# Up-projection token operands formed without GpSimd arithmetic, and halves of all tiles squared and scaled early for the last norms

## The chip, the cores and the metric

The kernel runs on one core of one Trainium2 chip. The metric is the device time of one execution in microseconds (us), which is a little longer than the span from the first to the last profiled instruction. The engines are called by their short names here: PE is TensorE's matmul and PEld its weight load, DVE is VectorE, ACT is ScalarE, POOL is GpSimd, SP is SyncE. SP issues plain DMAs, POOL issues those that add to their destination.

## The reference, cut to what matters

One layer of an encoder on 1024 tokens of 1024 channels, then a last norm. The change is in the norms and in the feed-forward part; the three mixers are left out here.

```
def rmsnorm(x, g):
    inv = lax.rsqrt(jnp.mean(xf * xf, axis=-1, keepdims=True) + RMS_EPS)
    return xf * inv * g

h = h + ymix @ w_out
h = h + conv_ffn(rmsnorm(h, norm2_g), w_up, ffn_conv_w, ffn_conv_b, w_down)   # 1024 -> 2 x 2816 -> 1024
return rmsnorm(h, final_norm_g)

def conv_ffn(h, w_up, conv_w, conv_b, w_down):
    u = dwconv_centred(h @ w_up, conv_w, conv_b)      # width 3 along the tokens
    a, v = jnp.split(u, 2, axis=-1)
    return (jax.nn.gelu(a) * v) @ w_down
```

## The kernel before, in words

**Precision.** Every large product is made in three matmuls (`mm3`, L97): an operand is split into a high part, which ACT writes rounded (L87), and a low part, the rest, by one subtraction (L88, on DVE unless another engine is named). `dsplit` is the other way to the same pair: ACT writes the negated value into the low part, a DMA issued by POOL adds the value to it (L93), and ACT then writes the high part.

**Tokens.** The residual lives in eight tiles `h` of 128 tokens by 1024 channels. After the mixers each tile is normed (`normed`, by `token_rstd`: two squares with accumulated sums on ACT, `tot` and `ms` on DVE, a power on POOL, a scaling on DVE).

**Up-projection.** It is a Strassen-Winograd product: seven half-size products instead of eight for each of 22 blocks `j` of 128 gate and 128 value channels. Its token operands are B11 and B21 (made from tiles 0 to 3 by `Ffn.first`), and B22, T1 to T4 (made by `Ffn.second` for four channel groups `kt` from transposes on PE that land in PSUM banks `trp`). There are four single banks, and a set of transposes takes a bank each. T1 is B12 minus B11, T2 is B22 minus T1, T3 is B12 minus B22, T4 is B21 minus T2. Its weight operands are made by `gate(j)` and `value(j)`: two loads, four sums and differences of 128x512 (L1208 to L1211), and the splits into A1, A22, S2 and S3. `start(j)` makes products P1 and P2 (`p` in the profile, p1 and p2 here), `rest(j)` P3, P6, P7, P5, P4 in this order, and puts them together on DVE (L1247 to L1259); then come the convolution (L712, L718), the gelu and a product on POOL (L1265). A product is 12 matmuls of 128x512.

**The order.** PE's instructions stand in the order in which the program issues them. On DVE, ACT, POOL and SP a scheduler orders them when the program is built, by its own view of time and by given priorities. The program calls `start(0)`, one group of `second` after each of its two products, the same with `start(1)`, then `start(2)`, then `rest(0)`. The raw halves of `second` (b22, t1, t2, t3) and z share six buffers of 128x512.

**Down-projection.** Again Strassen-Winograd, in two chunks `c` of seven products `p` with 6 and 5 steps: each step splits two blocks (tiles `dw`, on ACT and DVE) and uses them for four token tiles. Between them stand the sums of blocks (L1305) and the evacuations of PSUM into `h` (L1370). At the end of the second chunk, product 5 finishes the upper right half of tiles 0 to 3, which are then normed and stored (`final`), and the right half of tiles 4 to 7 is squared and multiplied by the gain on POOL (`done`, L1377). Product 6 finishes the left half of tiles 4 to 7, and `last` norms and stores them.

## Time and profile before

| | |
|---|---|
| time, median of 3 runs | 1168.62 us (1168.1 to 1172.08) |
| profiled execution | 1171.44 us, span 1169.7 us |
| PE | 1080.7 us, 92% of the span |
| PEld | 876.9 us, 75% |
| DVE | 988.4 us, 85% |
| ACT | 545.3 us, 47% |
| POOL | 338.2 us, 29% |
| granted TensorE clock, mean | 0.963 of full speed |

Busy shares are averages over very different stages. The up-projection's operands are made from about 479 to 528 us, the blocks run until about 930 us, the down-projection until the end. "Idle before, <-" in a row names what ended the engine's wait just before the group, with the time waited; x is the number of instructions.

### The profile page before, as it was taken

The page shows a single profiled execution, that of the slowest core. Times are in us where ns is not written, and L with a number is a line of the kernel's source. Part 1 is how long each engine was busy: PE and PEld are TensorE (multiplying, and loading weights), DVE is VectorE, ACT ScalarE, POOL GpSimd, SP SyncE. Part 2 cuts the span into 40 slices and gives each one's busy share as a digit, 9 for nine tenths or more (in the row PEclk, how much of TensorE's full clock was granted, in tenths as well). Part 3 has the DMA queues.
Part 4 walks back from the last instruction along what each step waited for, and adds up shares of the span by engine and source line. Part 5 has one row for each costly group of instructions (what it writes and reads, how often), then busy time and mean ns, then how long its engine had stood idle before and what let it go on. Part 6 is the DMA issues. An engine that isn't in the chain of part 4 may idle for free.

```text
span 1169.7 us, 13490 instructions
## 1 busy us (share of the span) xinstructions
PE 1080.7 (92%) x4938; PEld 876.9 (75%) x4938; DVE 988.4 (85%) x1289; ACT 545.3 (47%) x763; POOL 338.2 (29%) x282
## 2 busy tenths in 40 slices
PE   5899889989898899779899999999999989999896
PEld 4687678777677788658788888888888867887785
DVE  6885888997799966988898988888888799578975
ACT  6369567663243522633334343434343353545443
POOL 6021110103246342565332323232324062011002
PEclk9899989999899999979999999999999998999998
DMA  6287754447263542202222122222221771454003
GB/s 255 57 199 176 191 134 121 112 129 275 80 227 126 163 142 90 73 25 83 93 80 89 76 92 74 88 77 89 74 89 74 268 270 36 163 134 83 1 2 144
DMA packets 61103, 138.99 MB, mean 119 GB/s; under 512 B 11211, under 2 KB 19787, under 8 KB 61036
## 3 DMA queue, kind: packets, MB, share of 16 engines
q1 hardware_dynamic: 53116, 114.00, 28.1%
q0 software_dynamic: 7920, 24.12, 9.4%
q8 instruction: 39, 0.64, 0.2%
q14 instruction: 28, 0.23, 0.1%
HBM read 96.24 MB, written 30.33 MB: 108 GB/s over the span
## 4 chain that ended last, share of the span: by engine, by line
PE 48%; DVE 25%; issue 12%; DMA 6%; ACT 6%; POOL 4%; POOLq 0%; DVEq 0%; SPq 0%; ACTq 0%
PE p L97 30%; PE dn L97 6%; PE wo L97 4%; DVE dr L1305 2%; DVE dw L88 2%; DVE G L475 1%; DMA wn<-ox 1%; DVE G L473 1%; DMA dr<-gd 1%; PE xa L97 1%; PE ub L97 1%; DVE T L1165 1%; POOL rs L103 1%; DVE S L88 1%; DVE n L682 1%
## 5 line engine op out<-in xcount | busy, mean ns | idle before, releaser
L97 PE MATMUL dn<-dw 128*128 128x512 f32 x924 | 216.4, 396 | 9.3 <-DVE dw L88 9.2
L97 PEld LDWEIGHTS dn<-dw 128*128 128x128 f32 x924 | 176.1, 191 | 49.4 <-DVE dw L88 12.2
L97 PE MATMUL p<-T,S 128*128 128x512 f32 x792 | 187.5, 394 | 3.0 <-DVE T L1165 3.0
L97 PEld LDWEIGHTS p<-T,S 128*128 128x128 f32 x792 | 149.5, 189 | 37.4 <-DVE T L1165 3.4
L87 ACT ACTIVATE dw<-dr 128x512 fp32r<-128x512 f32 x154 | 88.2, 624 | 107.7 <-PE dn L97 93.7
L97 PE MATMUL p<-B,A 128*128 128x512 f32 x528 | 130.1, 401 | 6.1 <-ACT b L1171 4.1
L97 PEld LDWEIGHTS p<-B,A 128*128 128x128 f32 x528 | 100.4, 191 | 30.9 <-ACT b L1171 4.3
L88 DVE TENSOR_TENSOR dw<-dr,dw 128x512 fp32r<-128x512 f32 x154 | 101.8, 709 | 24.1 <-ACT dw L87 24.1
L1209 POOL TENSOR_TENSOR upv<-upv,upg 128x512 f32<-128x512 f32 x22 | 48.1, 2188 | 194.3 <-DVE upv L1208 194.0
L97 PE MATMUL wo<-wo,y 128*128 128x512 f32 x384 | 95.7, 410 | 8.0 <-DVE ms L635 4.3
L97 PEld LDWEIGHTS wo<-wo,y 128*128 128x128 f32 x384 | 75.0, 197 | 27.1 <-DVE ms L635 5.0
L1265 POOL TENSOR_TENSOR cv<-cv 128x1024 f32<-128x1024 f32 x22 | 76.7, 3485 | 60.1 <-DVE cv L718 47.5
L87 ACT ACTIVATE S<-upg 128x1024 fp32r<-128x1024 f32 x22 | 23.3, 1060 | 121.1 <-DVE upg L1211 109.3
L718 DVE SCALAR_TENSOR_TENSOR cv<-uv,cols,cv 128x1023 f32<-128x1023 f32 x44 | 75.1, 1707 | 0.8
L97 PE MATMUL p<-B,S 128*128 128x512 f32 x264 | 66.2, 400 | 4.6 <-ACT b L1171 3.8
L97 PE MATMUL p<-T,A 128*128 128x512 f32 x264 | 66.8, 402 | 2.9 <-DVE z L1251 2.9
L97 PEld LDWEIGHTS p<-B,S 128*128 128x128 f32 x264 | 50.4, 191 | 17.3 <-ACT b L1171 4.2
L97 PEld LDWEIGHTS p<-T,A 128*128 128x128 f32 x264 | 50.6, 192 | 15.4 <-DVE z L1251 3.4
L1305 DVE TENSOR_TENSOR dr<-dr 128x1024 f32<-128x1024 f32 (+1 forms) x48 | 53.1, 1127 | 6.1 <-DMA dr<-gd 6.1
L88 DVE TENSOR_TENSOR A<-upg,A 128x1024 fp32r<-128x1024 f32 x20 | 58.2, 2910 | 0.0
L718 DVE SCALAR_TENSOR_TENSOR cv<-ug,cols,cv 128x1023 f32<-128x1023 f32 x44 | 56.2, 1278 | 0.7 <-ACT cv L712 0.7
L103 POOL TENSOR_TENSOR rs<-ms,c_mhalf 128x1 f32<-128x1 f32 x24 | 14.3, 597 | 118.3 <-DVE ms L635 114.3
(383 smaller groups left out, 2049.8 us busy)
## 6 DMA issues: line engine op xcount, KB each, us to landing
upg<-in_w_up SPq DMA_DIRECT2D x22, 512.0 KB, 3.3
upv<-in_w_up SPq DMA_DIRECT2D x22, 512.0 KB, 3.4
gd<-cv SPq DMA_DIRECT2D x22, 512.0 KB, 2.6
dr<-gd SPq DMA_DIRECT2D x20, 512.0 KB, 9.0
dr<-in_w_down SPq DMA_DIRECT2D x20, 512.0 KB, 8.5
x<-in_x SPq DMA_DIRECT2D x8, 512.0 KB, 7.1
dft<-in_dftf POOLq DMA_DIRECT2D x8, 512.0 KB, 9.2
wor<-in_w_out SPq DMA_DIRECT2D x8, 512.0 KB, 6.8
```

The source lines that it names most:

```text
L87: self.nc.scalar.activation(hi, raw, AF.Identity)
L88: return (eng or self.nc.vector).tensor_tensor(lo, raw, hi.bitcast(F32), op=ALU.subtract).ins
L97: mm = lambda *a, **b: self.nc.tensor.matmul(*a, **b, **kw)
L103: self.last_pow = self.nc.gpsimd.tensor_tensor(out, base, expo, op=ALU.pow).ins
L473: V.tensor_tensor_scan(o[0:64, 1:512], r[0:64, 0:511], x[0:64, 0:511], initial=0.0, op0=ALU.mult, op1=ALU.add)
L475: V.tensor_tensor_scan(o[64:128, 510::-1], r[64:128, 511:0:-1], x[64:128, 511:0:-1], initial=0.0, op0=ALU.mult, op1=ALU.add)
L682: nc.vector.scalar_tensor_tensor(nT[1][kt][:, s], ps, self.c(gname, kt), nT[0][kt][:, s].bitcast(F32), op0=ALU.mult, op1=ALU.subtract)
L718: k.nc.vector.scalar_tensor_tensor(o[:, dst], ps[:, src], w, o[:, dst], op0=ALU.mult, op1=ALU.add)
L1165: eng.tensor_tensor(op[1], raw, f(op[0]), op=ALU.subtract)
L1209: G.tensor_tensor(a21, a21, a11, op=ALU.subtract)
L1265: G.tensor_tensor(o[0], o[0], o[1], op=ALU.mult)
L1305: self.k.nc.vector.tensor_tensor(B(o), B(x), B(y), op=f)
```

## The change

Six edits.

1. `second` also transposes tiles 0 to 3 (16 transposes a group instead of 8, in four banks instead of two). B11 is read afresh from PSUM (t3), T1 is one subtraction from PSUM instead of two, T3 is B11 minus T2 and T4 is B21 from PSUM minus T2, each one operation of DVE. POOL's subtractions and additions there are gone.
2. T1's low part is made by `dsplit` instead of on POOL.
3. `gate(1)` and `gate(2)` use `dsplit` instead of POOL's subtraction; S3 of blocks 0 and 1 uses `dsplit` instead of DVE's.
4. `value(j)`: the four sums of blocks 0, 1 and 2 go to DVE. Block 3 keeps all four on POOL, later blocks keep two and two.
5. `token_rstd`: the mean is taken by the square's scale, so one DVE operation of 128x1 stands in place of two (all norms).
6. The last norms: the left half of tiles 0 to 3 is squared and multiplied by the gain on DVE during product 3 of the second chunk, the right half of tiles 4 to 7 on DVE beside product 5. `final` then scales one half on DVE and the other on ACT for all eight tiles, with a store of 256 KB for each half.

```
-        halves = 1 if ssq is not None else 2
+        halves = (0, 1) if ssq is None else (half,)
-        tot = k.sm.tile([P, 1], F32, name="tot", bufs=4)
-        k.nc.vector.tensor_tensor(tot, ssq[:, 0:1], ssq[:, 1:2], op=ALU.add)
-        self.rstd(r, tot, L, (P, 1))
+        k.nc.vector.scalar_tensor_tensor(ms, ssq[:, 0:1], 1e-6, ssq[:, 1:2], op0=ALU.add, op1=ALU.add)
+        k.pow(r, ms, k.col(-0.5, "c_mhalf"))
...
         for kt in range(4):
-            p12, p22 = self.transposes(ns, kt), self.transposes(ns, kt + 4)
+            p22, p12 = self.transposes(ns, kt + 4), self.transposes(ns, kt)
+            p11, p21 = self.transposes(first, kt), self.transposes(first, kt + 4)
+            nc.scalar.activation(t3, p11, AF.Identity, scale=g1)
             nc.scalar.activation(b22, p22, AF.Identity, scale=g2)
-            V.scalar_tensor_tensor(t1, p12, g1, f(self.B11[kt][0]), op0=ALU.mult, op1=ALU.subtract)
-            V.scalar_tensor_tensor(t3, p12, g1, b22, op0=ALU.mult, op1=ALU.subtract)
-            split(self.B22[kt], b22, V)
-            V.tensor_tensor(t1, t1, f(self.B11[kt][1]), op=ALU.subtract)
+            V.scalar_tensor_tensor(t1, p12, g1, t3, op0=ALU.mult, op1=ALU.subtract)
             V.tensor_tensor(t2, b22, t1, op=ALU.subtract)
-            split(self.T2[kt], t2, V)
-            split(self.T3[kt], t3, V)
-            split(self.T1[kt], t1, G)
-            G.tensor_tensor(t2, f(self.B21[kt][0]), t2, op=ALU.subtract)
-            G.tensor_tensor(t2, t2, f(self.B21[kt][1]), op=ALU.add)
-            split(self.T4[kt], t2, V)
+            k.split(*self.B22[kt], b22)
+            k.split(*self.T2[kt], t2)
+            V.tensor_tensor(t3, t3, t2, op=ALU.subtract)
+            V.scalar_tensor_tensor(t2, p21, g2, t2, op0=ALU.mult, op1=ALU.subtract)
+            k.split(*self.T3[kt], t3)
+            k.dsplit(*self.T1[kt], t1)
+            k.split(*self.T4[kt], t2)
...
-        k.split(h, l, g, k.nc.gpsimd if j in (1, 2) else None)
+        (k.dsplit if j in (1, 2) else k.split)(h, l, g)
...
-        V = k.nc.vector if j > 3 else G
+        V, G = (k.nc.gpsimd if j in js else k.nc.vector for js in ((3,), range(3, self.NF)))
...
-            k.split(h, l, r)
+            (k.dsplit if j < 2 and r is v else k.split)(h, l, r)
...
+        def early(t, half):
+            x = h[t][:, 512 * half:512 * half + 512]
+            ssq[t] = k.sm.tile([P, 2], F32, name="ssqf", bufs=8)
+            net.square(ssq[t], half, x)
+            V.tensor_tensor(x, x, net.fg[:, 512 * half:512 * half + 512], op=ALU.mult)
+        def final(t, half):
+            r = net.token_rstd(h[t], ssq[t], half)
+            for i in (half, 1 - half):
+                if i == half:
+                    V.scalar_tensor_tensor(x, x, r, net.fg[:, s], op0=ALU.mult, op1=ALU.mult)
                 else:
+                    nc.scalar.activation(x, x, AF.Identity, scale=r)
+                nc.sync.dma_start(net.O["out"][P * t:P * t + P, s], x)
...
+            if c and p == 3 and q < 4:
+                early(q, 0)
...
-            net.final(i, h[i])
-            done(i)
+            early(4 + i, 1)
+            final(i, 1)
...
+            with k.tc.high_priority(400):
+                evac(1, 6, i, ps[i])
             with k.tc.high_priority(200):
-                evac(1, 6, i, ps[i])
-                last(i)
+                final(4 + i, 0)
```

**Place 1: DVE, where `second` begins (group kt 0).** Before, from the first read of the transposes; trp_4159 holds channels of B12, the t tiles are raw halves, and T1 to T4, B22 operands:

```order
L1173 SCALAR_TENSOR_TENSOR t1_4171<-trp_4159,cols_72,B11_4071 128x512 [waits PE_49]
L1174 SCALAR_TENSOR_TENSOR t3_4172<-trp_4159,cols_72,b22_4169 128x512 [waits Activation_49]
L1176 TENSOR_TENSOR t1_4171<-t1_4171,B11_4071 128x512 [waits DVE_49]
L1165 TENSOR_TENSOR B22_4149<-b22_4169,B22_4149 128x512 [waits DMASW2_49,DMASW0_49,Activation_49]
L1178 TENSOR_TENSOR t2_4178<-b22_4169,t1_4171 128x512 [waits DMASW4_49,DVE_49]
L1165 TENSOR_TENSOR T3_4155<-t3_4172,T3_4155 128x512 [waits Activation_49]
L1173 SCALAR_TENSOR_TENSOR t1_4216<-trp_4204,cols_72,B11_4071 128x512 [waits DVE_49,PE_49]
```

After, the same engine and place, until the next group's t1:

```order
L1197 TENSOR_TENSOR upv_4224<-upv_4224 128x512 [waits DMASW5_49,DVE_49]
L1198 TENSOR_TENSOR upv_4224<-upv_4224,upg_3928 128x512 [waits DVE_49]
L1166 SCALAR_TENSOR_TENSOR t1_4150<-trp_4133,cols_72,t3_4149 128x512 [waits Activation_49]
L1199 TENSOR_TENSOR upg_3928<-upv_4224,upg_3928 128x512 [waits DVE_49]
L1167 TENSOR_TENSOR t2_4151<-b22_4148,t1_4150 128x512 [waits DMASW4_49,DVE_49,Activation_49]
L88 TENSOR_TENSOR B22_4118<-b22_4148,B22_4118 128x512 [waits DMASW2_49,DMASW0_49,Activation_49]
L1200 TENSOR_TENSOR upg_3928<-upg_3928 128x512 [waits DVE_49]
L1170 TENSOR_TENSOR t3_4149<-t3_4149,t2_4151 128x512 [waits DVE_49]
L88 TENSOR_TENSOR T2_4120<-t2_4151,T2_4120 128x512 [waits Activation_49]
L1171 SCALAR_TENSOR_TENSOR t2_4151<-trp_4143,cols_72,t2_4151 128x512 [waits DVE_49,PE_49]
L88 TENSOR_TENSOR S2_4233<-upg_3928,S2_4233 128x1024 [waits Activation_49]
L1166 SCALAR_TENSOR_TENSOR t1_4205<-trp_4188,cols_72,t3_4204 128x512 [waits DMASW0_49,Activation_49]
```

The four sums of `value(0)` (upv, upg) moved onto DVE between the steps, and the next group's t1 now waits for a DMA issued by POOL (DMASW0).

**Place 2: DVE, block 3 of the up-projection (z frees PSUM for the next product, upg is a sum for the next block's S2).** Before:

```order
L1247 TENSOR_TENSOR ug_4713<-p12_4670,z1_4695 128x512 [waits Activation_49]
L88 TENSOR_TENSOR A1_4699<-upg_4697,A1_4699 128x1024 [waits DMAHW0_49,Activation_49]
L1211 TENSOR_TENSOR upg_4697<-upg_4697 128x512 [waits Pool_49]
L1251 TENSOR_TENSOR z1_4695<-p6_4717,z1_4695 128x512 [waits PE_49]
L1252 TENSOR_TENSOR ug_4713<-p3_4716,z1_4695 128x512 [waits DVE_49]
```

After:

```order
L1236 TENSOR_TENSOR ug_4725<-p12_4682,z1_4707 128x512 [waits Activation_49]
L88 TENSOR_TENSOR A1_4711<-upg_4709,A1_4711 128x1024 [waits DMAHW0_49,Activation_49]
L1240 TENSOR_TENSOR z1_4707<-p6_4729,z1_4707 128x512 [waits DMASW5_49,DVE_49,PE_49]
L1241 TENSOR_TENSOR ug_4725<-p3_4728,z1_4707 128x512 [waits DVE_49]
L1200 TENSOR_TENSOR upg_4709<-upg_4709 128x512 [waits Pool_49]
```

The sum that waits for POOL moved behind the two operations that free PSUM banks.

**Place 3: DVE, product 3 of the second chunk of the down-projection.** What the change puts between the splits (dw) and the sums (dr):

```order
L88 TENSOR_TENSOR dw_8694<-dr_7777,dw_8694 128x512 [waits Activation_49]
L1366 TENSOR_TENSOR h_7229<-h_7229,fg_8069 128x512 [waits Activation_49]
L88 TENSOR_TENSOR dw_8281<-dr_7431,dw_8281 128x512 [waits Activation_49] x2
L1366 TENSOR_TENSOR h_7230<-h_7230,fg_8069 128x512 [waits Activation_49]
L1366 TENSOR_TENSOR h_7231<-h_7231,fg_8069 128x512 [waits Activation_49]
L1366 TENSOR_TENSOR h_7232<-h_7232,fg_8069 128x512 [waits Activation_49]
L88 TENSOR_TENSOR dw_8302<-dr_7434,dw_8302 128x512 [waits Activation_49] x2
L1294 TENSOR_TENSOR dr_7431<-dr_7431,dr_7899 128x1024 [waits DVE_49]
L1294 TENSOR_TENSOR dr_7431<-dr_7899,dr_7431 128x1024 [waits DVE_49]
L88 TENSOR_TENSOR dw_8323<-dr_7780,dw_8323 128x512 [waits Activation_49]
L1294 TENSOR_TENSOR dr_7434<-dr_7434,dr_7902 128x512 [waits DVE_49]
L88 TENSOR_TENSOR dw_8323<-dr_7428,dw_8323 128x512 [waits Activation_49]
```

The four early products of h and fg stand ahead of the first split of product 4 (dw_8323); before, the row had the same splits, the two sums of 128x1024 and both sums of 128x512 ahead of it.

## Rows read from the trace of the kernel before

**Rows 1.** The page: its span and instructions.
```profile
span 1169.7 us, 13490 instructions
```

**Rows 2.** Busy time by stretch: PE, PEld, DVE, ACT, POOL, granted clock, DMA.
```profile
479.50:528.50 49.00, 35.36 (x142) 27.25 (x141) 44.74 (x43) 21.39 (x33) 34.46 (x21) 0.86 0.12 37
495.00:500.00 5.00, 2.24 (x5) 1.64 (x6) 5.00 (x5) 1.79 (x3) 3.21 (x1) 0.66 0.60 200
```

**Rows 3.** Timeline of PE, 476 to 532 us: start, length, what, [wait before].
```profile
476.73 3.04 PE L97 MATMUL p<-B,A 128*128 128x512 f32 x12
...
490.61 1.03 PE L1141 MATMUL trp<-ident,h 128*128 128x128 f32 x8
495.69 0.50 PE L97 MATMUL p<-B,A 128*128 128x512 f32 x1 [4.05 <-ACT b L1171]
498.26 7.98 PE L97 MATMUL p<-B,A 128*128 128x512 f32 x23 [2.06 <-POOL A L88]
...
520.73 7.95 PE L97 MATMUL p<-T,S 128*128 128x512 f32 x27 [2.97 <-DVE T L1165]
...
531.32 0.86 PE L97 MATMUL p<-B,S 128*128 128x512 f32 x3
```

**Rows 4.** The last link on DVE of the chain of waits, 476 to 560 us.
```profile
519.98 0.70 DVE T L1165
```

**Rows 5.** DVE's groups by line and form, 479.4 to 528.1 us: busy, mean ns.
```profile
L1165 DVE TENSOR_TENSOR T<-t,T 128x512 fp32r<-128x512 f32 x12 | 11.0, 931 | 1.4 <-ACT T L1164 1.4
L1165 DVE TENSOR_TENSOR B<-b,B 128x512 fp32r<-128x512 f32 x4 | 7.0, 1762 | 0.0
L1176 DVE TENSOR_TENSOR t<-t,B 128x512 f32<-128x512 f32 x4 | 6.1, 1526 | 0.0
L1178 DVE TENSOR_TENSOR t<-b,t 128x512 f32<-128x512 f32 x4 | 5.2, 1308 | 0.0
```

**Rows 6.** Timeline late in the down-projection, POOL idle: splits alone.
```profile
1120.26 8.51 DVE L88 TENSOR_TENSOR dw<-dr,dw 128x512 fp32r<-128x512 f32 x14
1121.58 3.39 ACT L87 ACTIVATE dw<-dr 128x512 fp32r<-128x512 f32 x6 [0.37 <-DVE dw L88]
```

**Rows 7.** Adding DMAs: `dsplit`'s of 512 KB (line 93), then tile wn's.
```profile
DMA to landing us min/median/max: 4.5/5.5/6.8
...
DMA to landing us min/median/max: 3.3/4.6/12.9
```

**Rows 8.** Timeline of blocks 3 and 4 of the up-projection, 570 to 600 us.
```profile
572.87 3.11 DVE L88 TENSOR_TENSOR A<-upg,A 128x1024 fp32r<-128x1024 f32 x1
...
577.42 0.69 DVE L1211 TENSOR_TENSOR upg<-upg 128x512 f32<-128x512 f32 x1 [1.44 <-POOL upg L1210]
578.03 0.68 DVE L1251 TENSOR_TENSOR z<-p,z 128x512 f32<-128x512 f32 x1
...
578.77 4.50 PE L97 MATMUL p<-T,A 128*128 128x512 f32 x12 [2.94 <-DVE z L1251]
...
591.47 8.44 PE L97 MATMUL p<-T,S 128*128 128x512 f32 x36
```

**Rows 9.** Timeline of product 3, second chunk of the down-projection.
```profile
1093.62 8.72 PE L97 MATMUL dn<-dw 128*128 128x512 f32 x30 [2.94 <-DVE dw L88]
1096.49 3.56 DVE L1305 TENSOR_TENSOR dr<-dr 128x1024 f32<-128x1024 f32 x4
```

**Rows 10.** Timeline of the end, 1100 to 1170 us.
```profile
1099.68 59.03 PE L97 MATMUL dn<-dw 128*128 128x512 f32 x257
...
1149.90 2.35 DVE L1114 SCALAR_TENSOR_TENSOR h<-h,rs,fg 128x1024 f32<-128x1024 f32 x1 [0.66 <-POOL rs L103]
...
1161.82 0.68 DVE L1370 TENSOR_TENSOR h<-dn,h 128x512 f32<-128x512 f32 x1
...
1163.48 0.15 DVE L635 TENSOR_SCALAR ms<-tot 128x1 f32<-128x1 f32 x1
...
1164.37 0.75 DVE L1384 SCALAR_TENSOR_TENSOR h<-h,rs,fg 128x512 f32<-128x512 f32 x1 [0.73 <-POOL rs L103]
```

More of the change, by code (lines that the diff above doesn't have):

```diff
@@ L636, in rstd, with square, token_rstd @@
         k.pow(out, t, bc(k.col(-0.5, "c_mhalf"), *shape))
-    def token_rstd(self, h, ssq=None):
+    def square(self, ssq, i, h):
+        self.k.nc.scalar.activation(self.k.half("sq"), h, AF.Square, scale=L ** -0.5, accum_out=ssq[:, i:i + 1])
+    def token_rstd(self, h, ssq=None, half=0):
         k = self.k
-        halves = 1 if ssq is not None else 2
+        halves = (0, 1) if ssq is None else (half,)
         if ssq is None:
             ssq = k.sm.tile([P, 2], F32, name="ssq", bufs=4)
-        for i in range(halves):
-            s = slice(512 * i, 512 * i + 512)
-            k.nc.scalar.activation(k.half("sq"), h[:, s], AF.Square, accum_out=ssq[:, i:i + 1])
-        tot = k.sm.tile([P, 1], F32, name="tot", bufs=4)
-        k.nc.vector.tensor_tensor(tot, ssq[:, 0:1], ssq[:, 1:2], op=ALU.add)
-        r = k.sm.tile([P, 1], F32, name="rs", bufs=4)
-        self.rstd(r, tot, L, (P, 1))
+        for i in halves:
+            self.square(ssq, i, h[:, 512 * i:512 * i + 512])
+        ms, r = (k.sm.tile([P, 1], F32, name=n, bufs=4) for n in ("tms", "rs"))
+        k.nc.vector.scalar_tensor_tensor(ms, ssq[:, 0:1], 1e-6, ssq[:, 1:2], op0=ALU.add, op1=ALU.add)
+        k.pow(r, ms, k.col(-0.5, "c_mhalf"))
         return r
@@ L1109, in mix_out @@
             yield i
-    def final(self, i, h):
-        k = self.k
-        r = self.token_rstd(h)
-        k.nc.vector.scalar_tensor_tensor(h, h, r, self.fg, op0=ALU.mult, op1=ALU.mult)
-        k.nc.sync.dma_start(self.O["out"][P * i:P * i + P], h)
 class Ffn:
@@ L1153, in first, with second @@
             k.nc.vector.scalar_tensor_tensor(lo, ps, g, hi.bitcast(F32), op0=ALU.mult, op1=ALU.subtract)
-    def second(self, ns):
+    def second(self, first, ns):
         k = self.k
-        nc, V, G = k.nc, k.nc.vector, k.nc.gpsimd
+        nc, V = k.nc, k.nc.vector
         self.B22, self.T2, self.T1 = (self.operand(n, "p2") for n in ("B22", "T2", "T1"))
         self.T3, self.T4 = (self.operand(n, "p") for n in ("T3", "T4"))
-        f = lambda x: x.bitcast(F32)
-        def split(op, raw, eng):
-            nc.scalar.activation(op[0], raw, AF.Identity)
-            eng.tensor_tensor(op[1], raw, f(op[0]), op=ALU.subtract)
@@ L1199, in value @@
         k = self.k
-        G = k.nc.gpsimd
         A, g = self.A[j], self.raw.pop(j)
@@ L1370, in evac @@
                 V.tensor_tensor(o, ps, o, op=ALU.add)
-        def done(i):
-            b = h[4 + i][:, 512:]
-            ssq[i] = k.sm.tile([P, 2], F32, name="ssq", bufs=4)
-            nc.scalar.activation(k.half("sq"), b, AF.Square, accum_out=ssq[i][:, 1:])
-            G.tensor_tensor(b, b, net.fg[:, 512:], op=ALU.mult)
-        def last(i):
-            b = h[4 + i]
-            r = net.token_rstd(b, ssq[i])
-            for e, s in ((V, slice(0, 512)), (None, slice(512, 1024))):
-                if e:
-                    e.scalar_tensor_tensor(b[:, s], b[:, s], r, net.fg[:, s], op0=ALU.mult, op1=ALU.mult)
-                else:
-                    nc.scalar.activation(b[:, s], b[:, s], AF.Identity, scale=r)
-                nc.sync.dma_start(net.O["out"][512 + P * i:512 + P * i + P, s], b[:, s])
-        ssq = [None] * 4
+        def early(t, half):
[6 more added lines that the diff above has]
+            for i in (half, 1 - half):
+                s = slice(512 * i, 512 * i + 512)
+                x = h[t][:, s]
+                if i == half:
+                    V.scalar_tensor_tensor(x, x, r, net.fg[:, s], op0=ALU.mult, op1=ALU.mult)
+                else:
+                    nc.scalar.activation(x, x, AF.Identity, scale=r)
+                nc.sync.dma_start(net.O["out"][P * t:P * t + P, s], x)
+        ssq = [None] * 8
         for g in range(2):
@@ L1707, in program @@
         ffn.gate(1)
-    second = ffn.second(h[4:])
+    second = ffn.second(h[:4], h[4:])
     for part in ffn.start(0):
```

4 lines of the change are left out of this document (1 added, 3 removed).

## The prediction

> **What bounds the kernel now.** I read the page first, then busy time in stretches of 5 us, then PE's timeline where a stretch shows PE idle, then what ended those waits. Over most of the span PE is busy without a gap, so only four places can move the time: the making of the token operands, one block behind it, product 3 of the second down-projection chunk, and the end.
>
> In the first place DVE is the bound. From 479.5 to 528.5 us DVE is busy 44.7 of 49.0 us and POOL 34.5, while PE has 35.4 [rows 2], some of it at the lower clock: 0.66 in the mean of 495 to 500 us, so part of that stretch at 1.2 instead of 2.4 GHz. PE's waits for operands end at 495.7, 498.3 and 520.7 us, among others [rows 3], and the chain of waits runs along DVE until the last T2 half at 519.98 [rows 4]. Only from 520.7 is PE dense again. I measure this place from the first product of block 0 at 476.73 to the first of P3 of block 1 at 531.32: 54.6 us [rows 3].
>
> Why DVE is slow there: alone, 14 splits take 8.51 us, a pitch of 0.61 us [rows 6]. Here the same form with two operands in SBUF takes 0.93, 1.76, 1.53 and 1.31 us in four groups [rows 5]. Those 24 instructions take 29.3 us; at 0.61 they would take 14.6. POOL is working beside them all the time [rows 2].
>
> **Part by part, first the token operands (edits 1 to 4).** POOL's arithmetic leaves this place, so I price DVE there at 0.61 us for 128x512 and twice 0.61, less the fixed part, some 1.15 us, for 128x1024. DVE has eight operations a group before and after; it gains the four sums of blocks 0 and 1 (8 x 0.61 = 4.9 us) and loses two S3 halves (2.3 us). DVE work alone would thus fall by some 12 us (14.7 - 2.6), if nothing new made it wait. Something does, so I follow the order row by row.
>
> The first group has 16 transposes now, and 8 take 1.03 us [rows 3]. They begin at 479.6, where the first product ends, so the first t1 can start at about 482.0: 1.6 us for twelve of them and some 0.7 for ACT's t3. The next group's t1 waits for the DMA that completes this group's T1 (DMASW0 in place 1). On that loop lie t1, t2, ACT's T2 half, ACT's negated T1 half and the DMA: 0.75 + 2 x 0.61 + 2 x 0.55 = 3.1 us plus the landing time L. ACT's 0.55 is 3.39 us over 6 [rows 6]. In the second loop ACT has T3, T4, B22 and the negated half ahead: 2.6 us plus L. DVE's own rows fill 6.0 us of the first loop (eight of 0.61 and one of 1.15) and 7.3 of the second (twelve).
>
> L is not shown for this tile. The nearest rows are `dsplit`'s own 512 KB, 4.5 to 6.8 us, median 5.5, and tile wn's 256 KB, the same size as here, 3.3 to 12.9, median 4.6 [rows 7]. I take 5.2, between the two medians, and keep 3.3 and 6.8 as ends; 12.9 is a rival. With 5.2 the loops take 8.3 and 7.8 us, and group 2's t1 starts at 498.1. Eight DVE rows later the last bank of group 2 is read, at about 503.9. PE then makes the last four transposes (0.5 us) and seven products without a wait: P1 and P2 of block 2, P3, P6, P7, P5, P4 of block 0. A product takes 2.81 us at full clock: three take 8.44 us in a dense block [rows 8]. So P3 of block 1 starts at 504.4 + 19.7 = 524.1. PE will have stood idle for some 4 us just before; after such waits it ran slow: 23 matmuls took 7.98 us instead of 5.4 [rows 3]. I add 2 us, between that 2.6 and nothing. 526.1 against 531.3: **-5.2 us**. With L at 3.3 DVE's rows bound both loops and it is -8.0, without the slow clock -10; with 6.8 it is -2.0.
>
> The added PE work is 32 transposes, 4.1 us [rows 3], in front of waits that are longer than that. If they were not covered, 4 us would come back. ACT gets eight more operations of 0.55 us and three negated ones of twice the width, some 7.5 us; it is busy 21.4 of 49 us [rows 2], and where its order matters, in the loops, it is counted.
>
> A rule of the Trainium skill speaks against this edit. It says in SBUF — State Buffer, section "SBUF: two separate sides", that a DMA issued by GpSimd needs descriptors which GpSimd cannot write while DVE holds the shared port pair, and gives 620 ns that became 3100 ns. By it L would grow by about 2.5 us and the two loops by 5, so this term would be near zero (an estimate from that page). The trace has both kinds of landing with DVE at work, and 6.8 us is the worst of 13 `dsplit` DMAs [rows 7]; I weigh it as the third rival. The page DMA: Bandwidth & Descriptors, section "Anatomy of one DMA — SWDGE (gpsimd) path", gives 2.0 us plus size over 436 GB/s, 2.6 us here, and by it the term would be -8.0; the rows show nothing that short.
>
> **Block 3 (place 2).** PE waits 2.94 us at 578.77 for z, and then runs 12 matmuls in 4.50 instead of 2.81 us [rows 8]. DVE reached z only at 578.03, since a sum ahead of it sat 1.44 us for POOL; A1 ahead of that took 3.11 us from 572.87. In the new order that sum stands behind z, which can start when A1 ends, at 576.0. PE would go on at 576.7 instead of 578.8, and with a wait under 1 us probably keeps its clock: 2.0 + 1.6. I take **-3.0**; ends 0, if DVE arrives as late for another reason, and -4.6.
>
> **All norms (edit 5).** One 128x1 operation less in each chain: 0.15 us [rows 10] and its hand-over, some 0.2. In the norms ahead of the up-projection and at the start most of it is beside other work: **-0.2**, ends 0 and -0.8.
>
> **Product 3 of the down-projection (edit 6, place 3).** PE resumes at 1093.62 and needs a new split pair every 2.81 us [rows 9]. The first pair of product 4 is due three steps later, at 1102.05. DVE ends its four sums at 1100.05 [rows 9] and needs 1.2 for the pair: 1101.3, so 0.8 us to spare. Four early products (4 x 0.61 = 2.44) come ahead, one 128x512 sum goes behind: 1103.1. PE stalls **+1.1** us; ends 0 and +2.4. The squares on ACT fall into its idle time.
>
> **The end (edit 6).** PE's last matmul ends at 1158.71, but the last evacuation starts at 1161.82 [rows 10]: DVE ran late behind the four whole-tile products of `final`, 2.35 us each (the last at 1149.90), two of them while POOL multiplied h and fg. From that evacuation to the end of the last scaling takes 3.30 us (1164.37 + 0.75 - 1161.82), and PE delivers a tile every 3.5 us (15 matmuls), so the lateness of 3.1 us was never made up. After, the scalings are 0.75 us, the early products stand where DVE waits for squares, and POOL only makes powers. A chain is 3.1 us and fits between two tiles; the last evacuation starts with PE's end. **-3.1 - 0.2 = -3.3**; ends -1.5, if half of the lateness stays, and -3.5. The 4.6 us of store and closing behind it stay.
>
> **The sum.** -5.2 - 3.0 - 0.2 + 1.1 - 3.3 = -10.6 us. The profiled execution took 1171.4 us for a span of 1169.7 [rows 1], so it would take 1160.8; the median is 2.8 us below that execution, and I put the same change on it: 1168.6 - 10.6 = **1158.0 us**.
>
> **The rivals.**
> *Most of the gain stays away.* Landing at 6.8 us (-2.0), block 3 unchanged (0), the stall at 2.4, the end at -2.5: -2.1 us, 1166.5. For it: both new waits on DMAs are in loops with no slack. Against: four separate terms at their bad end.
> *DVE alone bounds the operands.* L near 3.3 us, no slow clock, block 3 wholly gone: -10 - 4.6 - 0.4 + 1.1 - 3.5 = -17.4, 1151.2. For it: the DMA queues are nearly idle there, 12% [rows 2]. Against: waits of 4 us brought the lower clock each time [rows 2, 3].
> *The adding DMAs become the chain (slower).* Four T1 groups pass their buffers on through four landings in series, and P5 of block 0 needs the last: 482.0 + 13.3 (3.1, 2.6 and twice some 3.8 of DVE and ACT between landings) + 4 x L for its data, P3 of block 1 some 3.5 us later, after the rest of P5 and P4. With L = 12.9, the longest of wn's [rows 7], that is 550, 19 us later than now; with the other terms at -5.4 the time is 1182. It decides from L of about 8 us at this place (498.8 + 4 x 8.1 = 531.3) and 9.5 for the whole kernel; over 0.5% slower it is from 11. For it: one such landing, and the port rule cited above. Against: 13 of 13 `dsplit` landings are below 7.
>
> **How the numbers follow.** Forecast 0.60, its own range 1153 to 1163; little gain 0.15; the larger gain 0.18; slower 0.07. A measurement here can tell about 0.5%, 5.8 us, from no change. Faster by more than that (below 1162.8): 0.58 of the forecast, the larger gain 0.18 and a little of the small gain, 0.02, make 0.78. Within 0.5%: 0.15. Slower: the third rival with L above 11, 0.07. The range 1151 to 1166 leaves out the third rival, half of the larger gain and a little of the small one.
>
> **What would show it.** DVE's 128x512 operations in the operand stage at 0.6 to 0.8 us, and POOL with DMA issues alone until the first gelu product. First product to P3 of block 1 in 47 to 52 us. Landings of T1 at 4.6 to 6 us, with DVE waiting for them at t1 of groups 1 and 2. No wait of PE above 1.5 us at z of block 3. A new wait of about 1 us at the first step of product 4. The last evacuation within 0.2 us of PE's end. What would make it wrong: landings of 9 us or more, PE waiting for other things than transposes there, or new waits in blocks 1 and 2, where four sums were added to DVE.

## The result, and the profile after

The changed kernel takes 1155.36 us (median of 4 runs, 1153.17 to 1156.42) against 1168.63 us (4 runs, 1168.1 to 1172.08): ratio 0.9871, 95% interval 0.9852 to 0.9891, 13.3 us faster by the medians and 15.1 by the ratio. Beside other runs of before the same kernel came to 0.9869 (0.9846 to 0.9891).

First the page of the profile after, which answers to [rows 1]: its span. Then PE's timeline of the operand stage (start, length, what, [wait before and what ended it]), which answers to [rows 3].

```profile
span 1153.1 us, 13561 instructions
```

```profile
472.46 3.05 PE L97 MATMUL p<-B,A 128*128 128x512 f32 x12
...
482.91 0.66 PE L1137 MATMUL trp<-ident,h 128*128 128x128 f32 x4 [1.55 <-DVE t L1171]
...
489.52 0.66 PE L1137 MATMUL trp<-ident,h 128*128 128x128 f32 x4 [1.84 <-ACT t L1164]
...
498.95 1.11 PE L1137 MATMUL trp<-ident,h 128*128 128x128 f32 x4 [4.41 <-DVE t L1171]
499.72 7.68 PE L97 MATMUL p<-B,A 128*128 128x512 f32 x24
...
521.08 2.92 PE L97 MATMUL p<-B,S 128*128 128x512 f32 x12
```

From the first product of block 0 to P3 of block 1 it is 521.08 - 472.46 = 48.6 us, against 54.6. The waits are all at transposes now; behind the longest, 24 matmuls take 7.68 us instead of 5.6, at a granted clock of 0.50 from 499.7 to 503.5 us, so the lower clock came again.

Next DVE's groups by form in the same stage (busy us, mean ns | idle before), answering to [rows 5], the four starts of t1 from DVE's timeline, and what the view of tile T says of its adding DMAs, answering to [rows 7].

```profile
L88 DVE TENSOR_TENSOR T<-t,T 128x512 fp32r<-128x512 f32 x11 | 7.5, 687 | 1.2 <-ACT T L87 1.2
L1167 DVE TENSOR_TENSOR t<-b,t 128x512 f32<-128x512 f32 x4 | 2.7, 684 | 0.0
L88 DVE TENSOR_TENSOR B<-b,B 128x512 fp32r<-128x512 f32 x4 | 2.7, 682 | 0.0
```

```profile
477.64 0.75 DVE L1166 SCALAR_TENSOR_TENSOR t<-trp,cols,t 128x512 f32<-128x512 f32 x1 [0.35 <-ACT t L1164]
485.23 0.75 DVE L1166 SCALAR_TENSOR_TENSOR t<-trp,cols,t 128x512 f32<-128x512 f32 x1 [1.24 <-ACT t L1164]
493.09 0.74 DVE L1166 SCALAR_TENSOR_TENSOR t<-trp,cols,t 128x512 f32<-128x512 f32 x1
501.00 0.75 DVE L1166 SCALAR_TENSOR_TENSOR t<-trp,cols,t 128x512 f32<-128x512 f32 x1
```

```profile
DMA to landing us min/median/max: 3.3/3.3/3.9
```

The 128x512 subtractions, 0.93 to 1.76 us before, take 0.68. The landings took 3.3 to 3.9 us, not 5.2, and ended no wait: group 1's t1 waits for ACT, groups 2 and 3 start with no idle time on DVE. Busy times over the stage (PE, PEld, DVE, ACT, POOL, granted clock, DMA), answering to [rows 2], show POOL with DMA issues alone:

```profile
472.50:521.00 48.50, 40.66 (x198) 33.24 (x197) 36.56 (x56) 30.28 (x47) 6.26 (x8) 0.93 0.43 93
```

Block 3, from DVE's and PE's timeline, answering to [rows 8], and the end, answering to [rows 10]:

```profile
561.38 0.68 DVE L1240 TENSOR_TENSOR z<-p,z 128x512 f32<-128x512 f32 x1
562.09 0.69 DVE L1241 TENSOR_TENSOR ug<-p,z 128x512 f32<-128x512 f32 x1
...
565.00 0.69 DVE L1200 TENSOR_TENSOR upg<-upg 128x512 f32<-128x512 f32 x1 [2.22 <-POOL upg L1199]
...
565.68 2.97 PE L97 MATMUL p<-T,A 128*128 128x512 f32 x12
```

```profile
1079.56 65.14 PE L97 MATMUL dn<-dw 128*128 128x512 f32 x276 [2.98 <-DVE dw L88]
...
1144.74 0.69 DVE L1359 TENSOR_TENSOR h<-dn,h 128x512 f32<-128x512 f32 x1 [0.31 <-PE dn L97]
...
1147.10 0.75 DVE L1375 SCALAR_TENSOR_TENSOR h<-h,rs,fg 128x512 f32<-128x512 f32 x1 [0.66 <-POOL rs L103]
```

The sum now waits 2.22 us for POOL behind z, and PE has no wait there. The last evacuation starts 0.04 us after PE's end (1144.70), against 3.1 us before, and the last scaling ends 3.15 us after PE, against 6.41. The 276 matmuls from the wait in product 3 to PE's end took 65.09 us before (from 1093.62, [rows 9, 10]) and 65.14 now: no new stall in this profile.

### The profile page after: what moved, and what is told of

Read it like the earlier page. It is cut to its first block, busy times and chain, and to the rows that moved or that the text cites. A ratio compares the mean times of both kernels' runs of the same rounds, so it can differ in the third digit from the quotient of the medians.

```text
span 1153.1 us, 13561 instructions
## 1 busy us (share of the span) xinstructions
PE 1078.3 (94%) x4970; PEld 876.4 (76%) x4970; DVE 969.8 (84%) x1283; ACT 555.1 (48%) x779; POOL 296.7 (26%) x260
## 4 chain that ended last, share of the span: by engine, by line
PE 57%; DVE 25%; ACT 7%; DMA 6%; issue 4%; POOL 1%; SPq 0%; POOLq 0%; DVEq 0%; ACTq 0%
PE p L97 35%; PE dn L97 12%; PE wo L97 5%; DVE dw L88 3%; DVE dr L1294 2%; DMA dr<-gd 2%; DVE G L475 1%; DVE G L473 1%; DVE h L1359 1%; DVE n L684 1%; PE ub L97 1%; DMA wgr<-in_gates 1%; DVE q L720 1%; DVE h L1110 1%; DVE prm L460 1%
## 5 line engine op out<-in xcount | busy, mean ns | idle before, releaser
L97 PEld LDWEIGHTS dn<-dw 128*128 128x128 f32 x924 | 175.0, 190 | 51.2 <-DVE dw L88 14.4
L1198 POOL TENSOR_TENSOR upv<-upv,upg 128x512 f32<-128x512 f32 x19 | 43.0, 2266 | 191.9 <-DVE upv L1197 191.8
L103 POOL TENSOR_TENSOR rs<-tms,c_mhalf 128x1 f32<-128x1 f32 x24 | 15.1, 631 | 121.6 <-DVE tms L651 121.5
```

The lines of the kernel that those rows point to most:

```text
L97: mm = lambda *a, **b: self.nc.tensor.matmul(*a, **b, **kw)
L103: self.last_pow = self.nc.gpsimd.tensor_tensor(out, base, expo, op=ALU.pow).ins
L1198: G.tensor_tensor(a21, a21, a11, op=ALU.subtract)
```

## The experiments

Each time is the median of its runs; the ratio is to runs of before on the same chip at the same time. "Stage" is the stretch from the first product of block 0 to P3 of block 1, read from PE's timeline of each profile.

**One pair of rows.** The kernel before with two rows of DVE exchanged:

```
-        V.tensor_tensor(z, p6, z, op=ALU.add)
+        self.zl = V.tensor_tensor(z, p6, z, op=ALU.add).ins
...
+            if j == 4:
+                st.enter_context(k.tc.issue_after(self.zl))
             V.tensor_tensor(a12, a12, a11, op=ALU.subtract)
```

> The kernel before with two neighbouring rows of DVE exchanged: in block 3 the addition that makes z stands ahead of the sum of block 4 that waited 1.44 us for POOL. Nothing else moves on any engine. Theory (the wait for z is DVE's queue and nothing else): PE's wait of 2.94 us at z and the slow 12 matmuls behind it (4.50 us) go, 1168.6 - 4.4 = 1164.2 us. Rival (DVE reaches z late for another reason, or the gap comes back one block later): 1168 to 1169 us. For the first product of block 0, which came 4.3 us earlier in the changed kernel's profile than in that of before: if only edit 5 did that, it stands here near 476.7 us as in the profile of before; if the profile of before was merely a long execution, it can stand anywhere from 472 to 477.

Measured: 1166.76 us, ratio 0.9967 (0.9951 to 0.9983), 3.9 us less by the ratio and 2.5 by the medians. PE's timeline of blocks 3 and 4:

```profile
576.52 3.06 PE L97 MATMUL p<-T,A 128*128 128x512 f32 x12 [0.76 <-DVE z L1254]
579.42 5.76 PE L97 MATMUL p<-B,A 128*128 128x512 f32 x24
...
597.42 3.07 PE L97 MATMUL p<-T,A 128*128 128x512 f32 x12 [1.21 <-DVE z L1254]
```

The wait of 2.94 us [rows 8] became 0.76 and the 12 matmuls behind it run at full speed: 2.18 + 1.44 = 3.6 us won at block 3, of which block 4's z, 1.21 us late now, takes back 1.2 and 0.1 behind it, 2.3 us net. So the theory holds at its place, and a third of the gain goes one block later, as the rival has it. The first product of block 0 starts at 475.52 us.

**The end alone.** The kernel before with edits 5 and 6:

```
-            net.final(i, h[i])
-            done(i)
+            early(4 + i, 1)
+            final(i, 1)
```

> The kernel before with edits 5 and 6 alone (the norms' chain one operation shorter; early squares and products, half-tile scalings at the end). The operand stage and block 3 stay as they were. Theory (the parts of the change add up; the two traces show 3.26 us less between PE's last matmul and the last scaling, 0.67 us more behind it, no new stall in product 4): 1168.6 - 2.6 - 0.2 = 1165.8 us. Rival A (edit 5 is worth the 4 us by which the first product of block 0 came earlier): 1162 us, and the first product near 472.5. Rival B (the early products cost the stall of 1.1 us that I had forecast, and the profile after missed it): 1167 us.

Measured: 1164.76 us, ratio 0.9964 (0.9943 to 0.9984), 4.2 us less with 2 to 7 in its interval. In its profile the last scaling ends 3.14 us behind PE's end (before 6.41), but rival B's stall is there. PE's timeline from product 3 on:

```profile
1089.40 8.48 PE L97 MATMUL dn<-dw 128*128 128x512 f32 x36 [2.99 <-DVE dw L88]
1099.50 55.34 PE L97 MATMUL dn<-dw 128*128 128x512 f32 x240 [1.62 <-DVE dw L88]
```

The 36 matmuls are the three steps behind the wait that the kernel before has too. Here they run at full clock, and PE then waits 1.62 us for the first pair of product 4, which it does not do in the kernel before. The stage took 52.7 us. The time lies between the theory's and rival A's, so the parts add up as far as this can tell, and it cannot tell 1.6 us; the first product at 473.65 us speaks neither for rival A nor against it by itself.

**The change without its end.** Edit 6 undone in the changed kernel (`final`, `done` and `last` as before):

```
-            if c and p == 3 and q < 4:
-                early(q, 0)
```

> The changed kernel with the old end (edit 6 undone: whole-tile final scalings, no early products); operands, block 3 and norms as changed. Theory (parts add up: operands -6.0, block 3 -4.4, norms about 0 to -0.4): 1155.4 + 2.6 = 1158.0 us, with the last evacuation some 3 us behind PE's end again. Rival (the lateness at the end of before was caused by something that the other edits removed): 1155.4 us.

In this kernel the early squares of tiles 4 to 7 lack the mean's factor, which changes values and no work. Measured: 1158.42 us, ratio 0.9900 (0.9875 to 0.9925): 3 us above the changed kernel, as the theory has it, though the intervals overlap. The stage took 48.4 us. DVE's timeline at the end shows something that I had not priced:

```profile
1144.76 0.68 DVE L1364 TENSOR_TENSOR h<-dn,h 128x512 f32<-128x512 f32 x1
...
1147.79 0.68 DVE L1364 TENSOR_TENSOR h<-dn,h 128x512 f32<-128x512 f32 x1
...
1150.14 0.75 DVE L1378 SCALAR_TENSOR_TENSOR h<-h,rs,fg 128x512 f32<-128x512 f32 x1 [0.73 <-POOL rs L103]
```

PE ends at 1145.59 here and the last evacuation starts 2.2 us later, not 3.1: with edit 5 each of the chained tiles takes 3.03 us, where before they took 3.22 (two evacuations in the trace of before stand at 1158.60 and 1161.82). The last scaling ends 5.30 us behind PE, against 6.41 before: edit 5's 0.2 us is on the path once per late tile. In this order edit 5 brings 1.1 of the 3.26 us and edit 6 the other 2.15; edit 6 without edit 5 was not run.

**T1 on DVE.**

```
-            k.dsplit(*self.T1[kt], t1)
+            k.split(*self.T1[kt], t1)
```

> The changed kernel with T1's low part made by a DVE subtraction (as in its other operands), not by the negated copy on ACT and the adding DMA: four DMAs and four ACT copies less, four DVE operations of 0.6 us more. Theory A, my prediction's (a group's t1 waits for the landing of the adding DMA): the groups follow each other every 7.3 us instead of 7.9, time 1154 us or less. Theory B, from the trace after (landings of 3.3 us end no wait; ACT's queue bounds the second group, DVE's own rows the third): four operations of 0.61 us more on DVE, 1.2 to 2.4 us of them ahead of the last transposes, 1157 us.

Measured: 1153.69 us, ratio 0.9862 (0.9835 to 0.9888), not to be told from the changed kernel; the stage, though, took 51.2 us, 2.6 more. Theory A falls; B is right in the stage and wrong in the time. The rest of the profiled execution was shorter by 3.8 us than in the profile after, 1.1 of it ahead of the first product (471.31) and 2.6 behind the stage, where the kernel is the same. Two or three us are less than single medians here can tell apart, and from here on I judge the stage by its own length.

**The changed kernel again.** No edit.

> The changed kernel itself once more, beside the same runs of before as the next three. Theory (the stretch ahead of the up-projection varies between executions by some 4 us whatever the kernel, and the places of the change do not): first product of block 0 anywhere from 471 to 477 us, but from there to P3 of block 1 again 48.4 to 48.8 us, block 3 without a wait, and 3.2 us from PE's end to the last scaling; time 1155 to 1157 us. Rival (the profile that I read was a lucky one in the operand stage): that stretch is 50 us or more.

Measured: 1154.60 us, ratio 0.9869 (0.9846 to 0.9891); stage 48.55 us, no wait in block 3, the last scaling 3.15 us behind PE's end. These three places repeat within 0.1 us. Product 3 does not; PE's timeline there:

```profile
1079.13 8.49 PE L97 MATMUL dn<-dw 128*128 128x512 f32 x36 [2.99 <-DVE dw L88]
1088.63 55.32 PE L97 MATMUL dn<-dw 128*128 128x512 f32 x240 [1.01 <-DVE dw L88]
```

The same kernel, and now product 4's first pair is 1.01 us late: the stall that I had forecast and that the first profile did not have.

**Sums back on POOL.** Edit 4 undone in the changed kernel:

```
-        V, G = (k.nc.gpsimd if j in js else k.nc.vector for js in ((3,), range(3, self.NF)))
+        V, G = (k.nc.vector if j > 3 else k.nc.gpsimd), k.nc.gpsimd
```

> The changed kernel with the value sums of blocks 0 to 2 on POOL again, as in the kernel before (edit 4 undone); operands as changed. DVE has eight rows of 0.61 us less in the operand stage. Theory (POOL arithmetic beside DVE stretches DVE's rows, 0.93 to 1.76 us in the trace of before against 0.68 in that of after): DVE's 128x512 rows go over 0.9 us in the mean while POOL's sums of some 2.2 us run, and first product to P3 of block 1 takes 50.5 to 53 us instead of 48.6; time 1158 us. Rival (DVE's row count bounds the stage): the stage gets shorter by 2 to 3 us, 46 us, time 1153 us.

Measured: 1166.79 us, ratio 0.9974 (0.9956 to 0.9992). The stage took 55.0 us, longer than the theory's 50.5 to 53 and no shorter than before. The timeline of DVE and POOL in the first group, and PE behind the last group's transposes and in block 3:

```profile
479.30 1.30 POOL L1199 TENSOR_TENSOR upg<-upv,upg 128x512 f32<-128x512 f32 x1
479.61 1.53 DVE L1167 TENSOR_TENSOR t<-b,t 128x512 f32<-128x512 f32 x1
480.68 1.61 POOL L1200 TENSOR_TENSOR upg<-upg 128x512 f32<-128x512 f32 x1
...
481.07 1.76 DVE L88 TENSOR_TENSOR B<-b,B 128x512 fp32r<-128x512 f32 x1
482.63 0.90 POOL L93 DMA_DIRECT2D T<-t  x1 [0.35 <-PE trp L1137]
482.75 0.68 DVE L1170 TENSOR_TENSOR t<-t,t 128x512 f32<-128x512 f32 x1
...
484.14 0.75 DVE L1171 SCALAR_TENSOR_TENSOR t<-trp,cols,t 128x512 f32<-128x512 f32 x1
```

```profile
505.22 0.79 PE L97 MATMUL p<-B,A 128*128 128x512 f32 x1 [1.81 <-ACT t L1164]
507.61 7.33 PE L97 MATMUL p<-B,A 128*128 128x512 f32 x23 [1.59 <-DMA A<-upg]
...
576.04 4.61 PE L97 MATMUL p<-T,A 128*128 128x512 f32 x12 [2.93 <-DVE z L1240]
```

Beside a POOL sum a DVE row takes 1.53 and 1.76 us, without one 0.68, though DVE has eight rows less to do. That is not the whole of the 6.4 us by which the stage is longer: group 2's last bank is read only 2.2 us later after the first product than with the sums on DVE. The other 4.2 us come behind it, where PE waits 1.81 us for ACT's copy t3 and 1.59 us for the low part of block 2's A. ACT's two copies for that A stand later in its queue here, behind group 2's T1, so part of the loss is a new order on ACT. And block 3's wait is back, 2.93 us with 12 slow matmuls behind: with the sums on POOL, block 4's sum stands ahead of z on DVE again. So both terms, the operands' and block 3's, need edit 4.

**T1's low part on POOL.**

```
-            k.dsplit(*self.T1[kt], t1)
+            k.split(*self.T1[kt], t1, nc.gpsimd)
```

> The changed kernel with T1's low part subtracted by POOL (as before the change) in place of ACT's negated copy and the adding DMA: four POOL operations of 128x512 more, four ACT copies of 0.55 us and four DMAs less, DVE's rows unchanged. Theory (contention): DVE's rows beside those four stretch to 1 us and more, groups follow each other every 8.5 us or later, the stage is 50 to 52 us, time 1158 us. Rival (ACT's queue bounds the groups, POOL only hurts when it works all the time): ACT is relieved of 2.2 us, the stage is 47.5 us or less, time 1154 us.

Measured: 1156.94 us, ratio 0.9890 (0.9867 to 0.9913); stage 50.8 us, within the theory's range. The two rows of DVE that stretch, the longest operation of POOL, and what waits for it:

```profile
486.79 1.76 DVE L88 TENSOR_TENSOR B<-b,B 128x512 fp32r<-128x512 f32 x1
...
495.35 4.07 POOL L88 TENSOR_TENSOR T<-t,T 128x512 fp32r<-128x512 f32 x1 [1.77 <-ACT T L87]
...
499.45 0.69 ACT L1165 ACTIVATE b<-trp,cols 128x512 f32<-128x512 f32 x1 [2.61 <-POOL T L88]
...
500.19 8.56 PE L97 MATMUL p<-B,A 128*128 128x512 f32 x24 [2.18 <-ACT b L1165]
...
502.17 1.65 DVE L1167 TENSOR_TENSOR t<-b,t 128x512 f32<-128x512 f32 x1
```

Only two of DVE's 128x512 rows are stretched, by 2.05 us together. POOL's four operations take 1.35 to 4.07 us, and the longest runs beside rows of DVE that keep 0.68: there POOL is the one that is held up. It also holds a buffer, so that ACT's b22 of the last group waits 2.61 us for it, and PE 2.18 us for that. So the stage has the theory's length but not by the theory's reason alone: POOL's own delay stands in the chain, and the second of the two stretched rows comes only behind it.

**Only the sums.** The kernel before with edit 4 alone (the line shown for the sums back on POOL, the other way round).

> The kernel before with edit 4 alone: the value sums of blocks 0 to 2 on DVE instead of POOL. The operands stay as they were: T1's low part and T4's two additions on POOL, four gate splits there too, old norms, old end. DVE has eight rows of 0.61 us more in the operand stage, POOL eight of some 1.5 us less, and block 4's sum stands behind block 3's z. Theory (edit 4 is worth most of the operand term, since with the sums on POOL the changed kernel needs 55.0 us there, as much as before): stage 50 to 51 us, block 3 without a wait of over 1 us, time 1169 - 4 - 4 = 1161 us. Rival (as long as any arithmetic is left on POOL, DVE's rows stay long and eight more of them only add to it; edits 1 to 3 and 4 are worth something only together): stage 54 to 57 us, block 3's 4 us alone, time 1165 to 1167 us.

Measured: 1163.33 us, ratio 0.9952 (0.9932 to 0.9971). The stage took 53.6 us, among the 52.7, 54.6 and 55.7 of the three profiles with the old operands; block 3 has no wait. The window of the stage has the 49.4 us of DVE that it has in the kernel before (from 476.7 to 531.3 us), in 57 rows instead of 51:

```profile
474.00:527.50 53.50, 39.74 (x166) 31.02 (x165) 49.41 (x57) 23.51 (x36) 22.65 (x14) 0.89 0.13 40
```

That is the rival's mechanism: with POOL still at work for 22.65 us, six more DVE rows are paid by shorter ones, and nothing is won at the operands. The time came out between the two; block 3's 4 us are within its interval (3.4 to 7.9 us less).

**Block 1's value work late.** In the changed kernel block 1's value work stands behind the last operand group, and ACT's two copies for block 0's S3 behind the copy b22 of the second group, in `value`:

```
+            if j == 1:
+                st.enter_context(k.tc.issue_after(self.last2))
             A["A22"] = k.pair("w2", "A22", 512)
...
+                    if j == 0 and r is v:
+                        s2.enter_context(k.tc.issue_after(self.b22i))
```

> The changed kernel with two things moved: block 1's value work (its split of 128x512 and four sums on DVE, 5 x 0.61 us) stands behind the last operand group, and ACT's two copies for block 0's S3 (2.1 us) stand behind the second group's first two ACT rows. Theory (DVE's rows and ACT's queue bound the groups, not the landing of the adding DMA): groups follow each other every 6.4 to 6.9 us instead of 7.6 to 7.9, the last transposes come some 3 us earlier, PE's wait of 4.41 us there falls to about 2, first product to P3 of block 1 takes 45.5 us, time 1152.5 us. Rival A (the landing takes over at once as the bound, or S of block 1 is late and PE waits for it after P4 of block 0): the stage stays at 48 to 49 us, 1155.5 us. Rival B (the shorter wait also keeps PE at its full clock): 44 us, 1150.5 us.

Measured: 1153.15 us, ratio 0.9855 (0.9832 to 0.9879); stage 47.9 us, so rival A by the stage; the time is nearer to the theory's 1152.5, but not to be told from the changed kernel. DVE's t1 in groups 1 and 3, and PE:

```profile
483.77 0.75 DVE L1166 SCALAR_TENSOR_TENSOR t<-trp,cols,t 128x512 f32<-128x512 f32 x1 [0.47 <-DMA T<-t]
...
499.76 0.75 DVE L1166 SCALAR_TENSOR_TENSOR t<-trp,cols,t 128x512 f32<-128x512 f32 x1 [0.94 <-DMA T<-t]
```

```profile
496.97 1.11 PE L1137 MATMUL trp<-ident,h 128*128 128x128 f32 x4 [3.37 <-DVE t L1171]
497.74 8.26 PE L97 MATMUL p<-B,A 128*128 128x512 f32 x24
```

Now the landing does end DVE's waits: my loop existed, 0.8 us below what bounded the second group (starts 6.8 us apart against 7.6). And PE's wait is 1.0 us shorter, but the 24 matmuls behind it take 8.26 us instead of 7.68.

**PE's products moved up**, then **both moves**, then **both with T1 on DVE**:

```
-        ffn.gate(2)
-    for part in ffn.start(1):
-        next(second)
+    one, two = ffn.start(1), ffn.start(2)
+    next(one)
+    next(second)
+    next(one)
+    next(two)
     list(second)
-    list(ffn.start(2))
+    list(two)
...
             (k.dsplit if j < 2 and r is v else k.split)(h, l, r)
+            if j == 0 and r is g:
+                self.gate(2)
```

The second adds block 1's late value work (the two lines with `self.last2` above), the third T1's `k.split`.

> The changed kernel with another order on PE and in one pool: gate(2)'s weights take the pair that block 0's first products release (S3 of block 0 takes the later one), and PE has P1 of block 2 ahead of the last group's transposes and P2 behind them; before, both products stood behind all transposes. The arithmetic of every engine is the same. Theory (PE idles 4.4 us for DVE and then works off 24 matmuls that could have been done in that wait, at the lower clock): the wait at the last transposes falls to about 1.5 us, P3 of block 0 starts some 4.5 us earlier, first product to P3 of block 1 takes 44 us instead of 48.6; time 1150.5 us. Rival (the last B22, T2 or T3 halves are late then, or A of block 2 lands late, and PE waits for them instead): 47 to 48.6 us, time 1154 to 1155.5 us.

> The last kernel with block 1's value work on DVE (five rows of 0.61 us) behind the last operand group besides. Theory (with PE's products moved up, DVE's rows are the chain again, and five rows less of it are 3 us): first product to P3 of block 1 42 to 43 us, time 1149 us. Rival (the landing of T1, 3.3 us, is next in the loop, as where only that work was moved: 47.9 against 48.6 us): within 0.7 us of the last kernel, 43.5 to 44 us, or no gain.

> The kernel with PE's products moved up and block 1's value work late, and T1's low part subtracted by DVE instead of the adding DMA. DVE has nine rows a group (4 x 0.75 and 5 x 0.61 less overlap, some 5.7 us) and no operand buffer waits for a landing any more. Theory (in the two kernels with those moves DVE's remaining waits of 0.84 to 0.94 us, and ACT's, end with the landing of T1, so that loop is the bound): groups follow each other every 6 to 6.6 us instead of 7 to 9.9, first product to P3 of block 1 takes 42.5 to 44 us, time 1149.5 to 1151 us. Rival (the loop is bound by the copies on ACT and the six half buffers whoever makes T1): 46 us or more, time 1154 us, not to be told from the changed kernel.

Measured: 1154.86 us, ratio 0.9882 (0.9858 to 0.9907), stage 46.4; 1155.68 us, 0.9886 (0.9859 to 0.9913), 48.3; 1150.64 us, 0.9851 (0.9823 to 0.9879), 46.3. All three theories wanted a stage of 44 us or less and fall by it, though the last one's time lies where its theory had it, 1149.5 to 1151. PE's timeline of the last one:

```profile
488.10 0.72 PE L1137 MATMUL trp<-ident,h 128*128 128x128 f32 x4 [3.44 <-ACT t L1164]
488.52 7.38 PE L97 MATMUL p<-B,A 128*128 128x512 f32 x24
495.74 1.47 PE L1137 MATMUL trp<-ident,h 128*128 128x128 f32 x12
```

The wait moved to the third group's transposes, ahead of the products that I had moved, 24 matmuls run slow all the same, and the last group's transposes stand behind them: its t1 starts 9.95 us after the third's. This kernel has the lowest ratio of all; its interval overlaps the changed kernel's, so it beats the kernel before, and whether it beats the change is open.

## Why the prediction was right

The forecast was 1158.0 us and the measurement 1155.4, inside the range and on the right side. The four places were the right ones; part of the agreement in size is luck, as the steps show.

**Operands: right in size, half right in the reason.** Forecast -5.2, measured 48.6 - 54.6 = -6.0. DVE's rows fell to 0.68 us, one every 0.60 us, as priced, the wait that lowers the clock cost 7.68 - 5.6 = 2.1 us where I had put 2, and from the last bank of group 2 (498.9) to P3 of block 1 it was 22.2 us where the working gives 0.5 + 19.7 + 2 = 22.2. The step that failed is the one on the loops: L was 3.3 to 3.9 us, and the pitch of 7.6 to 7.9 us, which I had as 8.3 and 7.8, came from ACT's queue (S3's two copies of 1.05 us stand ahead of the next group's copy t3) and from DVE's own rows, waits included. One error hid the other: with L at 3.3 I had DVE alone at -8 to -10 and had left ACT's order out of it. (By the working's own rows that -8.0 should be -7.6: the first loop is then 3.1 + 3.3 = 6.4 us, longer than DVE's 6.0.) The landing bounds only once other work is moved away, as the late value work showed.

I had also put the gain down to all four edits alike. The runs show it as a product, not a sum: new operands with the sums on POOL 55.0 us, old operands with the sums on DVE 53.6, both together 48.4 to 48.6; T1 alone back on POOL 50.8. It does not follow POOL's busy time: 9.1 us of T1's arithmetic cost 2.2 us and 11.7 us of sums cost 6.4, since in each case a few rows, on DVE, ACT or POOL itself, stand in the chain. Edits 1 and 3 were not undone singly.

The sums on POOL show which rows suffer: those with both operands in SBUF (1.53 to 1.76 us), while t1 (L1166) and T4's raw half (L1171), with one operand in PSUM, keep 0.73 to 0.75 in every kernel. And it goes both ways: T1's subtraction on POOL took 1.35 us at best and 4.07 at worst. The Trainium skill says why in SBUF — State Buffer, section "SBUF: two separate sides": POOL and DVE share a port pair that is held exclusively for a whole instruction, and a DVE operation with two SBUF inputs needs it against a POOL operation that reads SBUF. The traces agree with that. The same page's starvation of POOL's DMA descriptors, which I had weighed against this edit, is told there of DVE in its two-port mode, and the page says that a `tensor_tensor` did not stall a DMA, so I had weighed it too high; here four landings of 3.3 to 3.9 us beside a DVE that is busy 36.6 of 48.5 us show none of it, and the third rival (L of 12.9) went with it.

**Block 3: right mechanism, too small.** Forecast -3.0, measured -4.6 (PE's starts stand 9.98 us earlier ahead of it and 14.62 behind it). Neither the wait nor the slow matmuls are left, the end of -4.6 that I had kept. The exchange of the two rows alone won 3.6 us at that place, so the queue was the cause; 1.3 of that came back one block later, which the new order does not have.

**Norms: counted once where they count per tile.** Forecast -0.2. Edit 5 alone takes 1.1 us off the late chain at the end, by the pitch of 3.03 against 3.22 us; I had its 0.2 us in the last chain only, and had not counted it once for each of the chained tiles, which I had in the rows. With edit 6 the tiles are not chained any more, so this 1.1 is part of the end's 3.3 and not on top of it.

**Product 3: the mechanism was right, the clock was left out.** Forecast +1.1. In the first profile after, it is 0 (65.14 against 65.09 us). DVE did come late: the last half of product 4's first pair starts at 1088.33 and ends at 1089.0, as worked out. But I let PE run at 2.81 us a step behind its wait of 2.98 us. The stretches behind that wait (PE busy and count, granted clock) show otherwise:

```profile
1079.60:1081.00 1.40, 1.40 (x5) 0.87 0.02 6
1081.00:1084.00 3.00, 3.00 (x9) 0.50 0.00 0
1084.00:1088.00 4.00, 4.00 (x19) 0.99 0.00 0
```

At 0.50, 1.2 of 2.4 GHz, PE lost some 1.6 us and needed the pair at about 1089.6. Before it did the same. I had counted the slow clock at the operands and at block 3 and not here, and in this profile it covered the new work.

Other profiles kept a granted clock of 1.00 behind the same wait of 2.98 to 2.99 us, and there the stall is at the place that I had named: 1.01 us in the changed kernel run again, 1.00 with the late value work, 1.62 with the end alone and 1.64 with both moves and T1 on DVE. Of the fourteen profiles five kept the clock and nine lost it for about 3 us. One of the five has the old end, the kernel before with edit 4 alone:

```profile
1084.68 63.51 PE L97 MATMUL dn<-dw 128*128 128x512 f32 x276 [2.98 <-DVE dw L88]
```

From the wait to PE's end the old end takes 63.51 us at full clock and the new end 64.8 to 65.4; behind a slow phase it is 65.1 and 65.1 to 65.4. So edit 6 costs 1.3 to 1.9 us here when the clock stays up, and 0 to 0.3 when it falls. That the first profile after showed none was luck.

**The end: right.** Forecast -3.3, measured 3.15 - 6.41 = -3.26, and the last evacuation stands with PE's end as I had it; less 0.67 us that the closing behind it took longer; that closing is 4.6 to 5.3 us over all these kernels, with the old end too (5.21 in the change without edit 6).

**The sum.** -6.0 - 4.6 - 3.3 + 0.7 + 0 is -13.2, with 0.7 us less between the first transposes and the first product, and 0.8 more in the rest (0.3 in block 2 and 0.7 where the down-projection starts and PE waits 1.41 us instead of 0.75, less 0.1 elsewhere): -13.1, or -13.0 before rounding. The 0.7 ahead of the first product had no term in the forecast: that piece takes 5.8 us in all ten profiles with the new norms and operands, 6.2 with the new norms alone and 6.5 to 7.9 with neither. The two profiled executions differ by 16.6 us: the other 3.6 lie ahead of the up-projection, where the transposes start at 466.63 instead of 470.24. The fourteen profiles have that start from 463.3 to 470.2 us, the two with the old code at 466.1 and 468.1 beside the 470.2 of before, and one with the new norms at 470.2: most of it is spread between executions, and no run here shows a part that edit 5 may have in it. The medians, 13.3 us apart, agree with the sum of the places. Of the rivals, the larger gain had its block 3 and its landing of 3.3 us right and its operands wrong; the other two did not come.

## What to carry to other kernels

Before you leave POOL arithmetic in a DVE-bound stretch, see which rows wait for it: with either half of the work left on POOL nearly all of the gain was gone (55.0 and 53.6 us), with T1's four subtractions there about a third (50.8). A mean of a group hides this; in that last kernel two rows of eight carried the higher means, and the longest row was POOL's own. Where a scheduler orders an engine's rows, look for a row that waits on another engine ahead of one that frees a buffer; one exchange was worth 3.6 us at its place, and moving the sums of other blocks had made it and undone it. Do not call a stall absent by one profile: behind the same PE wait of some 3 us the matmuls ran slow in nine executions and at full clock in five, and only in those could the late work show as a stall, 1.0 to 1.6 us in the four with the new end.
